# First stage of a one-core hybrid layer: a PSUM bank and a row buffer for each modulation block, the square-root table ahead of the tokens, two tiles' products side by side, and one scaling moved at the end

## The chip, the core and the metric

The kernel runs on one core of a Trainium2 chip. The metric is the device time of one execution in microseconds (us), and the kernel before takes 1265.78 us (median of 3 runs, 1265.62 to 1266.16). Everything is float32 at the interface. A matrix product is made of three products of rounded halves (high by high, high by low, low by high), so that three matmuls stand for one.

## What is computed

One layer of a diffusion backbone over 1024 latent tokens (8 tiles of 128) and 256 context tokens (2 tiles), model width 1024. The part that matters here is the beginning and the end:

```python
sh_a, sc_a, g_a, sh_f, sc_f, g_f = split(silu(c) @ w_ada + b_ada, 6)      # latent modulation
csh_a, csc_a, ...               = split(silu(c_ctx) @ w_ada + b_ada, 6)   # context modulation
hc = rmsnorm(ctx, norm_mix) * (1 + csc_a) + csh_a
hx = rmsnorm(x,   norm_mix) * (1 + sc_a)  + sh_a
u  = h @ w_in                      # its columns feed gates, attention q/k/v, mLSTM q/k/v/o
...                                # mLSTM heads, window attention, output projection
x  = x + g_f * conv_glu(modulate(rmsnorm(x, norm_ffn), sh_f, sc_f))
return rmsnorm(x, final_norm)      # per token: x / rms(x) * final_norm
```

## The kernel before, in words

**First stage** (lines 354 to 449; PE, DVE, ACT, POOL and SP follow the order of the source here, since all five are scheduled by hand). Tiles 0 and 1 are context, 2 to 9 latent. For each tile, `x_load` (L218) issues a load of 512 KB; `x_norm` squares and sums on ACT (L222), takes a root on ACT (L223) and scales on DVE (L224, L225); `x_trans` transposes on PE (L233), four blocks into each of two PSUM tiles `pt`; `x_evac` copies them into `xT`, the first half on ACT and the second on DVE (L238). Meanwhile the modulation is made in four blocks of 512 columns, numbered 0 and 1 (the two halves of the shift) and 2 and 3 (the two halves of the scale). A block is loaded in two pieces of 1 MB (`ada_load`, L258), multiplied in two steps (`ada_mm`, L269, q = 0 and 1), copied as four row groups from PSUM to the buffer `arow` by ACT (L271), and turned into columns by `ada_vec` with four small products (L278), after which DVE writes `modS` (blocks 0, 1) or `modG` (blocks 2, 3) (L281, L284).

`modulate(half, grp)` applies scale and shift to half of the eight 128-row slices of `xT`, for the context tiles (grp 0), latent tiles 2 to 5 (grp 1) or 6 to 9 (grp 2). It makes a rounded high part on ACT (L301, `hc` or `hl`), the full value on DVE or POOL (L298) and the low remainder on DVE (L303). `px_mm(c, K)` then multiplies tile c by the 272 columns `w_x`, for the slices of K0 = (1, 3, 0, 2) or K1 = (5, 7, 4, 6): for each slice high by high (L307), high by low (L308), low by high (L309). `px_out` takes the result away (L336 to L343). `spin(n)` (L352) issues n transposes whose result nobody reads.

Where things lie: `pas` holds the modulation's PSUM. Blocks 0 and 2 share one tile `pa` of two banks, and blocks 1 and 3 the next tile in the same place; products of tiles 6 and 7 are put into it too (`pas[-1]`). `arow` is one buffer for all four blocks. The pool `pl` has four banks for `pt`, `spin` and the products of tiles 2 to 5, 8 and 9. PE, ACT, DVE and POOL each run their instructions in order. DMAs are issued by SP in order, all on one queue.

**End** (the last product of the down projection, `m3`, four token blocks with 512 columns each). For block i, `after_m3` scales and adds the residual on DVE (L1956, L1484), squares on ACT (L1960) and takes a root (L2010). `end1` takes the reciprocal on DVE (L1967), scales columns 512 to 1023 on DVE (L1968) and 0 to 511 on ACT (L1969), and issues two output DMAs (L1972); one of the last block's two is issued by ACT itself. The list `plan` (L2078 to L2080) says what is issued after which block of matmuls (L2020).

Of the kernel before, what the change touches and what calls it, by code (L numbers as in the profile page):

```python
# [18 lines left out]
P = 128  # L19
D = 1024  # L20
KT = D // P
SEQ = 1024
# [56 lines left out]
def build(tc, I, out, dbg=None):  # L79
# [56 lines left out]
    def hsl(part, kt, c):  # L136
        if c < NC:
            return hc[part][:, kt, c * P:(c + 1) * P]
        c -= NC
        return hl[c // 4][part][:, kt, c % 4 * P:(c % 4 + 1) * P]  # L140
# [36 lines left out]

    pdk, pkk, plk, pa_ = (ExitStack() for _ in range(4))
    pd = pdk.enter_context(tc.tile_pool(name="pd", bufs=2, space=PSUM, side="right"))
    pk = pkk.enter_context(tc.tile_pool(name="pk", bufs=1, space=PSUM))  # L180
    pl = plk.enter_context(tc.tile_pool(name="pl", bufs=4, space=PSUM))
    xp = p1.enter_context(tc.tile_pool(name="xp", bufs=2))
# [11 lines left out]

    arow = ym[:, 1]
    scp = ym[:, 2, 0:32 * KT].rearrange("p (k j) -> p k j", k=KT)
# [65 lines left out]
    def ada_mm(n, q):  # L262
        if q == 0:
            if n in (0, 1):
                pas[-1] = pk.tile([P, SEQ], F32, name="pa", tag="pp")
            pas[n] = pas[-1][:, 512 * (n // 2):512 * (n // 2) + 512]
        pa, wa = pas[n], wps.pop((n, q))
        for k in range(4):
            T.matmul(pa[32 * k:32 * k + 32], scp[:, 4 * q + k], wa[:, k, :], start=q == 0, stop=q == 1)  # L269
        if q == 1:  # L270
            S.copy(arow, pa)  # L271

    was, wps = {}, {}

    def ada_vec(n):
        pm = pas[n][:, 0:8]
        for j in range(4):
            T.matmul(pm[:, 2 * j:2 * j + 2], arow[:, j * P:(j + 1) * P], sel[:], start=True, stop=True)  # L278
        half, dst = n % 2, (modS, modG)[n // 2]
        k4 = slice(4 * half, 4 * half + 4)  # L280
        V.tensor_tensor(out=dst[:, k4], in0=pm[:, 0:8].rearrange("p (j c) -> p j c", j=4),  # L281
                        in1=bc(spc(("bsh_a", "bsc_a")[n // 2], 4 * half, 4), 2), op=ALU.add)
        if n >= 2:
            V.scalar_tensor_tensor(out=dst[:, k4], in0=dst[:, k4], scalar=1.0, in1=bc(spc("nmix", 4 * half, 4), 2),  # L284
                                   op0=ALU.add, op1=ALU.mult)
# [35 lines left out]

    def px_mm(c, kts):
        if c not in pxs:
            if c in (6, 7):

                pxs[c] = pas[-1][:, 512 * (c - 6):512 * (c - 6) + 512]
            else:
                pool, tag = (pl, "l") if c >= 2 else (pd, "d")
                pxs[c] = pool.tile([P, 512], F32, name="px", tag=tag)
        px = pxs[c]  # L330
        for kt in kts:
            mm3(px[:, :XW], hsl(0, kt, c), hsl(1, kt, c), wX[0][:, kt, :], wX[1][:, kt, :], kt == K0[0], kt == K1[-1])

# [20 lines left out]
    with tc.manual_schedule(engines={mybir.EngineType.PE, mybir.EngineType.DVE, mybir.EngineType.Activation,  # L354
                                     mybir.EngineType.Pool}):
        with tc.manual_schedule(engines={mybir.EngineType.SP}):
            for c in range(6):
                x_load(c)
# [16 lines left out]
            x_trans(5); x_evac(5)  # L375
            ada_load(1, 0); ada_load(1, 1)
            wXf, wX = wX, wX((0,))
            ada_vec(0)
            spin(12)
            ada_mm(2, 0)  # L380
            ada_mm(2, 1)
            spin(5)
            ada_load(3, 0); ada_load(3, 1)
# [4 lines left out]
            modulate(0, 0)  # L388
            px_mm(0, K0)
            px_mm(1, K0)  # L390
            modulate(0, 1)
            x_norm(6)
            px_mm(2, K0)
            px_mm(3, K0)
            x_norm(7)
            x_trans(6); x_evac(6)
            ada_mm(1, 0)
            x_norm(8)
            x_trans(7); x_evac(7)
            x_norm(9)  # L400
            ada_mm(1, 1)
            x_trans(8); x_evac(8)
            ada_vec(1)
            ada_mm(3, 0)
# [44 lines left out]
        px_out(9)  # L449
    p0.close()  # L450


# [1512 lines left out]
    def end1(b):  # L1965
        o, r = os_[b], rn[b][:, 0:1]
        V.reciprocal(r, r)  # L1967
        V.scalar_tensor_tensor(out=o[:, 512:D], in0=o[:, 512:D], scalar=r, in1=fnr[:, 512:D], op0=ALU.mult, op1=ALU.mult)  # L1968
        S.activation(o[:, 0:512], o[:, 0:512], AF.Copy, scale=r)  # L1969
        for ns in halves[::-1]:  # L1970
            e = S if b == 3 and ns.start == 0 else nc.sync
            e.dma_start(out[b * P:(b + 1) * P, ns], o[:, ns])  # L1972
# [53 lines left out]
    for t, (p, ps, fresh) in enumerate(products):  # L2026
# [47 lines left out]
        if p == "m4":  # L2074

            part = lambda f_, *bs: [lambda b=b: f_(b) for b in bs]
            todo = [None] + todo
            plan = [todo[1:3], part(size2, 4, 5) + todo[3:4], part(size2, 6) + part(end2, 4, 5) + todo[4:5],  # L2078
                    part(size2, 7) + part(end2, 6) + part(after_m3, 0), part(end2, 7) + part(after_m3, 1) + part(end1, 0),
                    part(after_m3, 2) + part(end1, 1), part(after_m3, 3) + part(end1, 2, 3)]  # L2080
            todo = []
# [101 lines left out]
```

## Time and profile before

| what | value |
|---|---|
| time, median of 3 runs | 1265.78 us |
| time of the profiled execution | 1265.89 us |
| its span | 1264.1 us |
| PE busy | 1234.4 us (98%) |
| DVE, ACT, POOL busy | 972.8, 637.9, 187.1 us |
| first matmul starts | 9.39 us |
| last matmul ends | 1256.59 us |

The profile is of one execution. A row of the timeline gives start, length, engine, line, operation and how many instructions were merged; what stands in brackets is idle time before the row and what ended it. A matmul's length contains its way through the array, so that the distance from start to start is what a chain of matmuls pays for each. A row of the waits gives the time waited in all, how often, and the longest. A row of the DMA issues gives the median time from issue to landing.

### The profile page before, as it was taken

Reading aid. Unit: us, or ns where it says so; the run is one execution under the profiler, and the core shown is the slowest. Engines: PE = TensorE matmul, PEld = TensorE weight load, DVE = VectorE, ACT = ScalarE, POOL = GpSimd, SP = SyncE. Lnnn points to the kernel's source line nnn. Section 1 sums busy time; section 2 is a strip of 40 time slices with the busy share of each in tenths; the row PEclk is TensorE's granted clock in tenths of the full one; section 3 lists DMA queues with packets and bytes.
Section 4 is the critical chain, followed back from the end, with each engine's and each line's share of the span. In section 5 each row is a group of like instructions: output and inputs, shape, how many; then the busy total and the mean of one; then the engine's idle time right before and its main releaser. Section 6 shows DMA issues by size and latency. Waiting matters only on the chain.

```text
span 1264.1 us, 19253 instructions
## 1 busy us (share of the span) xinstructions
PE 1234.4 (98%) x7047; PEld 1060.2 (84%) x7047; DVE 972.8 (77%) x1691; ACT 637.9 (50%) x1309; POOL 187.1 (15%) x162
## 2 busy tenths in 40 slices
PE   6999999999999999999999999999999999999997
PEld 4799999999898888888887888888888888788886
DVE  5873777777787888788987877777777777877887
ACT  6632556464865777776843333333333334434435
POOL 1200000000001443221002232133231232001000
PEclk9999999999999999999999999999999999999999
DMA  9541535362354333104313322223322237975553
GB/s 361 184 142 34 145 115 153 115 181 75 85 175 160 134 120 115 51 34 167 117 51 130 115 99 102 95 102 117 103 105 100 93 135 269 335 250 187 195 192 134
DMA packets 90560, 176.17 MB, mean 139 GB/s; under 512 B 12954, under 2 KB 29538, under 8 KB 90466
## 3 DMA queue, kind: packets, MB, share of 16 engines
q1 hardware_dynamic: 90178, 174.15, 41.2%
q8 instruction: 56, 0.92, 0.3%
q10 hardware_dynamic: 288, 0.79, 0.2%
q14 instruction: 38, 0.31, 0.1%
HBM read 136.58 MB, written 38.33 MB: 138 GB/s over the span
## 4 chain that ended last, share of the span: by engine, by line
PE 84%; DVE 6%; ACT 5%; DMA 3%; issue 2%; POOL 1%; SPq 0%; ACTq 0%; DVEq 0%; POOLq 0%
PE pd L2020 14%; PE pa L1480 8%; PE pc L1480 8%; PE pp L588 7%; PE pe L1480 4%; PE pd L1480 4%; PE pb L1480 4%; PE u L1182 3%; PE pv L307 2%; PE pv L309 2%; PE pv L308 2%; PE po L307 2%; PE po L309 2%; PE po L308 2%; PE pt L1159 2%
## 5 line engine op out<-in xcount | busy, mean ns | idle before, releaser
L1597 ACT CAST wh<-Rb 128x1024 fp32r<-128x1024 f32 (+1 forms) x63 | 56.8, 903 | 144.1 <-PE pd L1480 77.1
L2020 PE MATMUL pd<-dh,al 128*128 128x512 f32 x296 | 115.4, 390 | 0.9 <-DVE al L1361 0.9
L2020 PE MATMUL pd<-dl,ah 128*128 128x512 f32 x296 | 115.3, 389 | 0.0
L2020 PE MATMUL pd<-dh,ah 128*128 128x512 f32 x296 | 115.1, 389 | 0.0
L1480 PE MATMUL pc<-hB,wh 128*128 128x512 f32 x344 | 105.6, 389 | 0.0
L1480 PE MATMUL pa<-hB,wh 128*128 128x512 f32 x336 | 103.8, 390 | 0.2 <-ACT sn L1679 0.2
L1198 DVE TENSOR_TENSOR wl<-Rb,wh 128x1024 fp32r<-128x1024 f32 (+1 forms) x63 | 65.8, 1045 | 39.2 <-ACT wh L1597 38.6
L1715 POOL TENSOR_TENSOR tt<-vt,tt 128x512 f32<-128x512 f32 x22 | 29.5, 1341 | 367.5 <-ACT tt L1709 367.5
L588 PE MATMUL pp<-hl,wh 128*128 128x512 f32 x256 | 79.3, 405 | 0.0
L307 PE MATMUL pv<-wh,hl 128*128 128x256 f32 x256 | 75.9, 296 | 0.0
L1480 PEld LDWEIGHTS pc<-hB,wh 128*128 128x128 f32 x344 | 64.6, 188 | 13.5
L1480 PEld LDWEIGHTS pa<-hB,wh 128*128 128x128 f32 x336 | 62.9, 188 | 14.1 <-ACT sn L1679 1.1
L309 PE MATMUL pv<-wh,hl 128*128 128x256 f32 x256 | 72.4, 283 | 0.0
L308 PE MATMUL pv<-wl,hl 128*128 128x256 f32 x256 | 72.3, 282 | 0.0
L2020 PEld LDWEIGHTS pd<-dh,al 128*128 128x128 f32 x296 | 55.6, 188 | 13.1 <-DVE al L1361 1.6
L1480 PE MATMUL pc<-hB,wl 128*128 128x512 f32 x172 | 66.4, 389 | 0.0
L2020 PEld LDWEIGHTS pd<-dl,ah 128*128 128x128 f32 x296 | 55.5, 188 | 11.8 <-DVE dl L1361 0.3
L1480 PE MATMUL pa<-hB,wl 128*128 128x512 f32 x168 | 65.4, 389 | 0.0
L2020 PEld LDWEIGHTS pd<-dh,ah 128*128 128x128 f32 x296 | 55.6, 188 | 11.6
L1166 ACT CAST ph<-pt 128x512 fp32r<-128x512 f32 (+1 forms) x88 | 46.2, 525 | 25.3 <-PE pt L1159 25.0
L1136 DVE TENSOR_REDUCE nm<-sps 128x1 f32<-128x641 f32 (+1 forms) x64 | 50.3, 786 | 4.9 <-PE sps L1132 3.4
L1480 PE MATMUL pd<-hB,wh 128*128 128x512 f32 x176 | 54.0, 390 | 0.0
(1082 smaller groups left out, 3694.4 us busy)
## 6 DMA issues: line engine op xcount, KB each, us to landing
w<-in_w_ada_dram SPq DMA_DIRECT2D x64, 256.0 KB, 2.8
br<-in_w_down_dram SPq DMA_DIRECT2D x25, 512.0 KB, 5.9
ar<-act_s SPq DMA_DIRECT2D x44, 256.0 KB, 4.0
Ra<-in_w_up_dram SPq DMA_DIRECT2D x21, 512.0 KB, 3.6
Rb<-in_w_up_dram SPq DMA_DIRECT2D x21, 512.0 KB, 3.6
act_a<-tt SPq DMA_DIRECT2D x33, 256.0 KB, 2.0
act_s<-tt SPq DMA_DIRECT2D x33, 256.0 KB, 2.0
wr<-in_w_h_dram SPq DMA_DIRECT2D x16, 512.0 KB, 4.1
```

The costliest lines, as they stand in the source:

```text
L307: T.matmul(ps, st_hi, mv_hi, start=first, stop=False)
L308: T.matmul(ps, st_hi, mv_lo, start=False, stop=False)
L309: T.matmul(ps, st_lo, mv_hi, start=False, stop=last)
L588: T.matmul(pp[:, 512 * n:512 * n + 512], wkq[sw][:, kt, cs], hl[n][part][:, kt, :], start=kt == 0 and sw + part == 0, stop=kt == KT - 1 an ...
L1136: V.tensor_reduce(out=self.nm[:, j:j + 1], in_=self.sv[j], axis=AX.X, op=ALU.max, negate=True)
L1166: S.copy(self.ph[i][:, :w], self.pt[i][:, :w])
L1182: T.matmul(self.u[:], vv[:, c, self.g], part[i][:, kk * 2 * P:(kk + 1) * 2 * P], start=kb + m == 0, stop=kb == last and m == 1)
L1198: sub = lambda e, o, x, y: e.tensor_tensor(out=o, in0=x, in1=y, op=ALU.subtract)
L1480: T.matmul(ps[:, cols], wt[sw][:, j, kt * P:kt * P + P], hB[part][:, blk, kt, cols], start=first and n == 0, stop=last and n == len(seq) - ...
L1597: S.copy(wt[0][:], src)
L1715: G.tensor_tensor(out=self.tt[:, h2_], in0=self.vt[:], in1=self.tt[:, h2_], op=ALU.mult)
L2020: T.matmul(ps[:], ac[sa][:, js], w[sw], start=first and n == 0, stop=last and n == 2, skip_group_check=not fresh)
```

## The change

Five edits, the first four in the first stage. (1) `pas[n]` becomes a one-bank tile of a new pool `pm_`, with one bank for blocks 0 and 1 and one for 2 and 3; tiles 6 and 7 take these banks over. Pool `pl` moves to the right side; pool `pk`, which held `pa`, is opened after the stage. (2) Block 2 gets its own row buffer. (3) An ACT activation with a square root stands ahead of the first tile. (4) The order on PE and DVE changes: `ada_vec(0)` and the first step of block 2 come before DVE's split of `w_x`, the number of spins falls from 12 + 5 to 8 + 6, two tiles are multiplied side by side (`px_two`), and blocks 1 and 3 are multiplied at other places between the transposes. (5) In the end, ACT's scaling is issued ahead of DVE's in `end1`, and `end1` of block 2 ahead of `after_m3` of block 3.

```diff
+    pm_ = pmk.enter_context(tc.tile_pool(name="pm_", bufs=1, space=PSUM))
+    pl = plk.enter_context(tc.tile_pool(name="pl", bufs=4, space=PSUM, side="right"))
...
-    arow = ym[:, 1]
+    arow = lambda n: ym[:, 7 if n == 2 else 1]
...
         if q == 0:
-            if n in (0, 1):
-                pas[-1] = pk.tile([P, SEQ], F32, name="pa", tag="pp")
-            pas[n] = pas[-1][:, 512 * (n // 2):512 * (n // 2) + 512]
+            pas[n] = pm_.tile([P, 512], F32, name="pa", tag=f"pa{n // 2}")
...
-                pxs[c] = pas[-1][:, 512 * (c - 6):512 * (c - 6) + 512]
+                pxs[c] = pas[2 * c - 11]
...
+    def px_two(cs, kts):
+        for kt in kts:
+            for c in cs:
+                px = px_bank(c)
+                T.matmul(px, hsl(0, kt, c), wX[0][:, kt, :], start=kt == K0[0], stop=False)
+                T.matmul(px, hsl(0, kt, c), wX[1][:, kt, :], start=False, stop=False)
+        for kt in kts:
+            for c in cs:
+                T.matmul(px_bank(c), hsl(1, kt, c), wX[0][:, kt, :], start=False, stop=kt == K1[-1])
...
+            S.activation(rstd[:, 0:1], spc("c4"), AF.Sqrt, bias=eps_t[:], scale=0.0)
             for c in range(6):
                 x_load(c)
...
             ada_load(1, 0); ada_load(1, 1)
+            ada_vec(0)
+            ada_mm(2, 0)
             wXf, wX = wX, wX((0,))
-            ada_vec(0)
-            spin(12)
-            ada_mm(2, 0)
+            spin(8)
             ada_mm(2, 1)
-            spin(5)
+            spin(6)
...
-            px_mm(0, K0)
-            px_mm(1, K0)
+            px_two((0, 1), K0)
             modulate(0, 1)
             x_norm(6)
-            px_mm(2, K0)
-            px_mm(3, K0)
+            px_two((2, 3), K0)
             x_norm(7)
+            ada_mm(1, 0)
             x_trans(6); x_evac(6)
-            ada_mm(1, 0)
             x_norm(8)
+            ada_mm(1, 1)
             x_trans(7); x_evac(7)
             x_norm(9)
-            ada_mm(1, 1)
+            ada_vec(1)
             x_trans(8); x_evac(8)
-            ada_vec(1)
             ada_mm(3, 0)
...
     p0.close()
+    pmk.close()
+    pk = pkk.enter_context(tc.tile_pool(name="pk", bufs=1, space=PSUM))
...
         V.reciprocal(r, r)
+        S.activation(o[:, 0:512], o[:, 0:512], AF.Copy, scale=r)
         V.scalar_tensor_tensor(out=o[:, 512:D], in0=o[:, 512:D], scalar=r, in1=fnr[:, 512:D], op0=ALU.mult, op1=ALU.mult)
-        S.activation(o[:, 0:512], o[:, 0:512], AF.Copy, scale=r)
...
-                    part(after_m3, 2) + part(end1, 1), part(after_m3, 3) + part(end1, 2, 3)]
+                    part(after_m3, 2) + part(end1, 1), part(end1, 2) + part(after_m3, 3) + part(end1, 3)]
```

Outside the places shown below, and the swap on DVE of block 0's `modS` with the split of `w_x`, each engine's instructions stand in the same order as before, to the end of the program; SP's order is the same throughout.

PE, where tiles 0 and 1 meet, before (`hc0` is the high part, `hc1` the low remainder; `px` with its number is the tile's PSUM):

```order
L307 MATMUL px_431<-wh_364,hc0_178 128x272
L308 MATMUL px_431<-wl_365,hc0_178 128x272
L309 MATMUL px_431<-wh_364,hc1_179 128x272
L307 MATMUL px_444<-wh_364,hc0_178 128x272
L308 MATMUL px_444<-wl_365,hc0_178 128x272
L309 MATMUL px_444<-wh_364,hc1_179 128x272
```

The same engine after, at the last slice of the high parts:

```order
L339 MATMUL px_430<-wh_375,hc0_178 128x272
L340 MATMUL px_430<-wl_376,hc0_178 128x272
L339 MATMUL px_433<-wh_375,hc0_178 128x272
L340 MATMUL px_433<-wl_376,hc0_178 128x272
L343 MATMUL px_430<-wh_375,hc1_179 128x272
L343 MATMUL px_433<-wh_375,hc1_179 128x272
```

Before, each slice's three products stand together and the second tile follows the first; after, the tiles alternate, and all products with the low remainder stand behind all those with the high part.

PE between the products of tile 3 and those of tile 4, before (`pt` transposes of tiles 6 to 9; `pa<-wa` block 1, `pa<-sel` its `ada_vec`, `pa<-wt` block 3):

```order
L233 MATMUL pt<-ident,xi 128x128 x8
L269 MATMUL pa<-wa,ym 32x512 x4
L233 MATMUL pt<-ident,xi 128x128 x8
L269 MATMUL pa<-wa,ym 32x512 x4
L233 MATMUL pt<-ident,xi 128x128 x8
L278 MATMUL pa<-sel,ym 128x2 x4
L269 MATMUL pa<-wt,ym 32x512 x4
L233 MATMUL pt<-ident,xi 128x128 x8
```

The same place after:

```order
L267 MATMUL pa<-wa,ym 32x512 x4
L233 MATMUL pt<-ident,xi 128x128 x8
L267 MATMUL pa<-wa,ym 32x512 x4
L233 MATMUL pt<-ident,xi 128x128 x8
L276 MATMUL pa<-sel,ym 128x2 x4
L233 MATMUL pt<-ident,xi 128x128 x8
L267 MATMUL pa<-wt,ym 32x512 x4
L233 MATMUL pt<-ident,xi 128x128 x8
```

Both steps of block 1 moved one tile ahead, `ada_vec(1)` stands ahead of tile 8, and tile 8 now lies between `ada_vec(1)` and the first step of block 3.

ACT at the very end, before (o_11163 is block 2 and o_11164 block 3; `jk` is the sum of squares):

```order
L1969 ACTIVATE o_11162<-o_11162,rn_11170 128x512
L1960 ACTIVATE jk_12767,rn_11172<-o_11164 128x512
L2010 ACTIVATE rn_11172<-rn_11172 128x1
L1969 ACTIVATE o_11163<-o_11163,rn_11171 128x512
L1969 ACTIVATE o_11164<-o_11164,rn_11172 128x512
```

After (o_11167 is block 2, o_11168 block 3):

```order
L1980 ACTIVATE o_11166<-o_11166,rn_11174 128x512
L1980 ACTIVATE o_11167<-o_11167,rn_11175 128x512
L1972 ACTIVATE jk_12776,rn_11176<-o_11168 128x512
L2022 ACTIVATE rn_11176<-rn_11176 128x1
L1980 ACTIVATE o_11168<-o_11168,rn_11176 128x512
```

The scaling of block 2 moved ahead of block 3's squares; DVE's reciprocal and scaling of block 2 move in the same way ahead of block 3's residual.

More of the change, by code (lines that the diff above doesn't have):

```diff
@@ L175, in load_split @@
         return rest
-    pdk, pkk, plk, pa_ = (ExitStack() for _ in range(4))
+    pdk, pkk, plk, pa_, pmk = (ExitStack() for _ in range(5))
     pd = pdk.enter_context(tc.tile_pool(name="pd", bufs=2, space=PSUM, side="right"))
-    pk = pkk.enter_context(tc.tile_pool(name="pk", bufs=1, space=PSUM))
-    pl = plk.enter_context(tc.tile_pool(name="pl", bufs=4, space=PSUM))
+    pm_ = pmk.enter_context(tc.tile_pool(name="pm_", bufs=1, space=PSUM))
+    pl = plk.enter_context(tc.tile_pool(name="pl", bufs=4, space=PSUM, side="right"))
     xp = p1.enter_context(tc.tile_pool(name="xp", bufs=2))
@@ L270, in ada_mm @@
         if q == 1:
-            S.copy(arow, pa)
+            S.copy(arow(n), pa[:])
     was, wps = {}, {}
@@ L277, in ada_vec @@
         for j in range(4):
-            T.matmul(pm[:, 2 * j:2 * j + 2], arow[:, j * P:(j + 1) * P], sel[:], start=True, stop=True)
+            T.matmul(pm[:, 2 * j:2 * j + 2], arow(n)[:, j * P:(j + 1) * P], sel[:], start=True, stop=True)
         half, dst = n % 2, (modS, modG)[n // 2]
@@ L320, in rotate, with px_bank @@
         V.tensor_tensor(out=sv(dst), in0=sv(dst), in1=sv(ta[:])[:, :, ::-1], op=ALU.add)
-    def px_mm(c, kts):
+    def px_bank(c):
         if c not in pxs:
             if c in (6, 7):
-                pxs[c] = pas[-1][:, 512 * (c - 6):512 * (c - 6) + 512]
+                pxs[c] = pas[2 * c - 11]
             else:
@@ L329, in px_mm @@
                 pxs[c] = pool.tile([P, 512], F32, name="px", tag=tag)
-        px = pxs[c]
+        return pxs[c][:, :XW]
+    def px_mm(c, kts):
+        px = px_bank(c)
         for kt in kts:
-            mm3(px[:, :XW], hsl(0, kt, c), hsl(1, kt, c), wX[0][:, kt, :], wX[1][:, kt, :], kt == K0[0], kt == K1[-1])
+            mm3(px, hsl(0, kt, c), hsl(1, kt, c), wX[0][:, kt, :], wX[1][:, kt, :], kt == K0[0], kt == K1[-1])
+    def px_two(cs, kts):
+        for kt in kts:
+            for c in cs:
+                px = px_bank(c)
+                T.matmul(px, hsl(0, kt, c), wX[0][:, kt, :], start=kt == K0[0], stop=False)
[3 more added lines that the diff above has]
+                T.matmul(px_bank(c), hsl(1, kt, c), wX[0][:, kt, :], start=False, stop=kt == K1[-1])
     def px_out(c):
```

## The prediction

> **What bounds the kernel now.** I read the page's busy shares first, then the windows of the stages that the edits touch, then the timeline of PE there, then what it waits for, and last the end. From the page:
>
> ```profile
> PE 1234.4 (98%) x7047; PEld 1060.2 (84%) x7047; DVE 972.8 (77%) x1691; ACT 637.9 (50%) x1309; POOL 187.1 (15%) x162
> ```
>
> The windows (PE busy, number, clock, share of the DMA engines, GB/s) show where the other 2% is:
>
> ```profile
> 10.00:28.30 18.30, 16.24 (x119) 1.00 1.04 396
> 28.30:36.20 7.90, 7.62 (x49) 1.00 1.04 390
> 36.20:45.00 8.80, 8.19 (x66) 1.00 0.96 351
> 53.80:75.00 21.20, 21.20 (x167) 1.00 0.32 100
> ```
>
> Up to 45 us the DMA engines are full at 390 to 400 GB/s; from 53.8 us on PE has no hole at all. So what counts is how early PE gets into the stretch after 53.8 us: whatever it gains until then is kept, since all later work follows in an unchanged order. Before that, a product can start no earlier than its piece of the modulation weights lands. The issues on SP, and the time from issue to landing of each of these four:
>
> ```profile
> 9.51 2.38 SPq L258 DMA_DIRECT2D wa<-in_w_ada_dram  x1
> 19.78 0.38 SPq L258 DMA_DIRECT2D wa<-in_w_ada_dram  x1
> 21.55 0.92 SPq L258 DMA_DIRECT2D wa<-in_w_ada_dram  x1
> 24.26 3.23 SPq L258 DMA_DIRECT2D wt<-in_w_ada_dram  x1
> ```
>
> ```profile
> wa<-in_w_ada_dram SPq DMA_DIRECT2D x1, 1024.0 KB, 14.7
> wa<-in_w_ada_dram SPq DMA_DIRECT2D x1, 1024.0 KB, 14.8
> wa<-in_w_ada_dram SPq DMA_DIRECT2D x1, 1024.0 KB, 15.8
> wt<-in_w_ada_dram SPq DMA_DIRECT2D x1, 1024.0 KB, 15.8
> ```
>
> Issue plus landing: block 2's second piece lands at 24.2, block 1's two at 34.6 and 37.35, block 3's first at 40.1 us. PE around them:
>
> ```profile
> 23.39 1.97 PE L269 MATMUL pa<-wa,ym 128*32 128x512 f32 x16 [0.48 <-DVE modS L281]
> 26.11 1.05 PE L278 MATMUL pa<-sel,ym 128*128 128x2 f32 x8
> 27.02 0.96 PE L352 MATMUL spin<-ident 128*128 128x128 f32 x7
> 28.32 0.40 PE L307 MATMUL px<-wh,hc 128*128 128x272 f32 x1 [0.34 <-ACT hc L301]
> ...
> 36.17 1.04 PE L233 MATMUL pt<-ident,xi 128*128 128x128 f32 x8
> 37.13 1.06 PE L269 MATMUL pa<-wa,ym 128*32 128x512 f32 x8
> 38.13 1.09 PE L233 MATMUL pt<-ident,xi 128*128 128x128 f32 x8
> 39.15 1.06 PE L269 MATMUL pa<-wa,ym 128*32 128x512 f32 x8
> 40.15 1.09 PE L233 MATMUL pt<-ident,xi 128*128 128x128 f32 x8
> 41.31 1.05 PE L278 MATMUL pa<-sel,ym 128*128 128x2 f32 x8
> 42.69 1.07 PE L269 MATMUL pa<-wt,ym 128*32 128x512 f32 x8 [0.33 <-DVE modS L281]
> 43.69 1.09 PE L233 MATMUL pt<-ident,xi 128*128 128x128 f32 x8
> 45.02 0.40 PE L307 MATMUL px<-wh,hl 128*128 128x272 f32 x1 [0.24 <-ACT xT L238]
> ```
>
> Block 2 (23.39) ends at 25.36: its second half of about 1.0 us starts at 24.3, as the weights land. Block 1's second step starts at 39.15, 1.8 us after its weights: there PE is late, not the DMA.
>
> **The change, part by part.** *Root table ahead.* The load that it takes away from between the first two tiles, and the hole in which it now lies:
>
> ```profile
> 5.59 1.06 ACT L222 ACTIVATE ym<-xi 128x1024 bf16<-128x1024 f32 x1 [2.43 <-DMA xi<-in_ctx_dram]
> ...
> 6.76 1.28 ACT L223 ACT_TABLE_LOAD   x1
> ```
>
> ACT waits 2.43 us for the first tile, which holds the 1.28 us load and one small activation. So the six tiles run 1.28 us earlier; but block 2 cannot end before 24.2 + 1.0 us, and it does so already. I count 0; without that cover it would be 1.28 us.
>
> *Own bank and row buffer, block 2's first step and `ada_vec(0)` ahead.* They take away the 0.48 us at 23.39. Block 2's first step now runs when its first piece lands, but the second ends at 25.3 as before. Again 0, with at most 0.1 us of gain. The three spins that go away stood in waits; the new row buffer's first other use is a DVE write after the products at 26.11 that read it. Nothing is lost there. PE will stand idle for about 1.3 us ahead of block 2's first piece and 0.7 us ahead of the second. The Trainium skill ("TensorE: Matmul & The Clock Gate", What's actually happening) says that the array falls to half its clock after an idle window of about 3.4 us; by that rule these holes cost nothing either, and the sum stays.
>
> *Two tiles side by side.* Before, the 48 products of tiles 0 to 3 go from 28.32 to 36.17, 7.85 us. Their pace without a wait, here also across a change of bank:
>
> ```profile
> 53.63 0.28 PE L309 MATMUL pa<-wh,hl 128*128 128x272 f32 x1
> 53.75 0.29 PE L307 MATMUL px<-wh,hc 128*128 128x272 f32 x1
> ```
>
> That is 0.125 us from start to start, 6.0 us for 48. What they wait for is the low remainder, once for each slice, first by DVE's own row and then by PE's waits:
>
> ```profile
> 31.89 2.48 DVE L303 TENSOR_TENSOR hl<-ym,hl 128x512 fp32r<-128x512 f32 x4
> ```
>
> ```profile
> PEld px L309 <- DVE hl L303: 1.2, 6, 0.3
> PEld pa L269 <- DMA wa<-in_w_ada_dram: 0.7, 1, 0.7
> ```
>
> The last remainder of tiles 2 and 3 is there at 31.89 + 2.48 = 34.37. Before, it feeds tile 2's last product, and all twelve of tile 3 (1.5 us) follow: 36.17. After, only two products of that slice are left, since the 16 with the high part run while DVE works: 34.37 + 0.04 + 2 x 0.125 = 34.65. Gain: 1.5 us. An alternation between two banks at every second product is not in the trace. Its pace is bounded by the 0.125 us above, and by the slow pace that PE shows at its start:
>
> ```profile
> 9.39 3.67 PE L233 MATMUL pt<-ident,xi 128*128 128x128 f32 x16 [9.39 <-DVE xi L225]
> 15.47 1.06 PE L233 MATMUL pt<-ident,xi 128*128 128x128 f32 x8 [0.51 <-DVE xi L225]
> ```
>
> There a transpose takes 0.23 us, later 0.13: 1.75 times as long, which would make 0.22 us of 0.125. I take 0.125, since one change of bank costs nothing; the other end is the third rival. A rule of the Trainium skill speaks for that other end (the same page, A second HAM failure mode: psum-queue depth-cycling): a kernel that cycles through PSUM banks lets PE stop so often that its clock falls again and again.
>
> *Order of blocks 1 and 3.* Step by step, with lengths from the rows above (a step or a tile's transposes 1.0 us from start to start, `ada_vec` 0.9): block 1's first step 34.65 (its weights landed at 34.6), tile 6 at 35.65 to 36.65. Then PE waits: the second step must not start before 37.4. What is queued behind it is all that follows on PE, tile 7 first; ACT and DVE wait for tiles 7 to 9. From there: tile 7 at 38.4, `ada_vec(1)` at 39.4, tile 8 at 40.3, block 3's first step at 41.3 (weights at 40.1), tile 9 at 42.2, where before it was 43.69. So 1.5 us are gained at tile 9, and the wait at 42.69 (0.33 us) is gone within this. Tile 9's second half waits perhaps 0.2 us for DVE's copy of tile 8, which now stands behind `modS`; ACT copies the first half, which releases tile 4's product: 45.02 - 1.5 = 43.5. From tile 4 on the order is the old one. Later, tile 6 no longer waits for `modG` (0.33 us before); but the products of tiles 2 and 3 with K1 wait for DVE's remainders, which hang on `modG` and moved by the same 1.5 us. So that bit is given back. The first stage gains 1.5 us, at least 1.0 (tile 9 late on DVE, or weights 0.4 us later) and at most 1.75 (39.15 to 37.4).
>
> *The end.* ACT's last rows, with the wait ahead of block 3's squares, DVE's first of block 3, and the landing of ACT's DMA:
>
> ```profile
> 1258.06 0.63 ACT L1960 ACTIVATE jk<-o 128x512 bf16<-128x512 f32 x1 [1.74 <-DVE o L1484]
> ...
> 1259.02 1.32 ACT L1969 ACTIVATE o<-o,rn 128x512 f32<-128x512 f32 x2
> 1260.37 0.37 ACTq L1972 DMA_DIRECT2D out_dram<-o  x1
> ```
>
> ```profile
> 1256.61 0.69 DVE L1956 TENSOR_TENSOR tm<-pd,gfr 128x512 f32<-128x512 f32 x1 [1.12 <-PE pd L2020]
> ```
>
> ```profile
> out_dram<-o ACTq DMA_DIRECT2D x1, 256.0 KB, 2.8
> ```
>
> The two scalings (1.32) are blocks 2 and 3; block 2's now lies in the hole of 1.74 us, and DVE's part of it (0.9 us) in that of 1.12 us. Block 3's can start when its reciprocal is there, some 0.3 us earlier (1259.3 instead of 1259.6). The last DMA then starts 0.3 us earlier, and the two of block 2 are out of its way. I count 0.35 us, between 0.1 (block 2's DVE part delays block 3's by 0.2) and 0.7 (the last landing at 2.3 instead of 2.8 us). The swap inside `end1` orders two engines that do not wait for each other: 0.
>
> *Sum.* The profiled execution took 1265.89 us, 0.11 more than the median. 1265.89 - 1.5 - 0.35 = 1264.04, less 0.11: **1263.9 us**.
>
> **The rivals.**
> - *The DMA queue does follow.* If the loads were bound by their issue, the 1.28 us of the root table would move all landings, and the caps at 24.2 and 37.35 with them: 1263.9 - 1.28 = 1262.6. For it: block 1's first load is issued (19.78) as soon as block 0's product has freed the buffer. Against it: the loads land 15 us after issue with the DMA engines at 1.04 all the while. 0.11.
> - *The lead is lost.* If a chain on DVE or ACT in the later stages, and not PE, sets the pace at some place, only the 0.35 us at the end and little else remain: 1265.4. Against it: 21.20 of 21.20 us busy from 53.8 on, and later DVE's inputs come from PE's products, which are early too. 0.16.
> - *PE falls to its slow pace in the side-by-side products*, which makes it slower. At 0.22 us, 48 products take 10.6 us and end at 38.9 instead of 34.65. Block 1's first step and tile 6 follow, so its second step starts at 40.9, or 41.4 if these two are slow in part; before, it was 39.15. 1265.8 + 2.0 - 0.35 = 1267.4; each further step of 1.0 us at the slow pace adds 0.75, so from the second on it is slower by over 0.2%. It decides from about half of the products on: the first 0.7 us fall into the wait for block 1's weights, and 1.85 more eat the gain. Against it: PE kept its pace over the present waits of this stretch (six of 0.3 us or less). The rule of the Trainium skill on cycling through banks (the page and section above) would give this time; this trace shows the slow pace at the start alone. 0.07.
>
> **How the numbers follow.** My forecast has 0.66. Its own bounds are -1.75 - 0.7 and -1.0 - 0.1: 1263.2 to 1264.8, to which 0.2 us for the spread of the runs comes. The range reaches over the lost lead, to 1265.5, and at the low side to 1262.9, a little short of the first rival (0.11); left out are that rival and the slow pace, 0.18 together, and what I do not see. A change of 0.2%, about what a measurement can tell, is 2.5 us: faster than 1263.25 are the first rival and a small part of the forecast (0.11 + 0.07), slower than 1268.3 most of the slow pace (0.05), and 0.77 lie between.
>
> **What would show it.** Right: in the changed profile the first root needs no table load, yet block 2 still ends at 25.3; PE's products of tile 3 end near 34.7; block 1's second step starts at its landing near 37.4; tile 4 starts near 43.5; the stretch from 53.8 to 75 us is shifted by 1.5 us; ACT's last scaling starts 0.2 to 0.3 us after the root before it, with no other scaling between. Wrong: landings of the modulation weights over 0.5 us earlier, products of 272 columns 0.2 us apart in the side-by-side stretch, a lead at 75 us that is gone at 400, or block 3's residual delayed at the end.

## The result and the profile after

The changed kernel takes 1264.76 us (median of 22 runs, 1263.32 to 1266.44), the kernel before beside it 1266.31 (22 runs, 1265.62 to 1269.23). The ratio is 0.9984, 95% interval 0.9978 to 0.9990: about 2.0 us, 0.16%. The medians alone lie 1.55 us apart, the sum foresaw 1.85. It is a gain, since the interval leaves out 1, but a smaller one than the 0.2% that the prediction took for what a measurement can tell. The profiled execution took 1263.85 us (span 1262.1), where the prediction's sum for such an execution was 1264.04; it was the fourth fastest of the 22, and the median lies 0.9 us above the 1263.9 of the prediction. Between the two profiled executions lie 2.04 us: 1.69 up to the last matmul and 0.35 behind it.

The page of the changed kernel, busy times:

```profile
PE 1233.2 (98%) x7044; PEld 1059.5 (84%) x7044; DVE 973.4 (77%) x1691; ACT 638.8 (51%) x1310; POOL 187.5 (15%) x162
```

The windows of the first stretch and of the one without a hole (PE busy and number first; clock, DMA share and GB/s last):

```profile
10.00:28.30 18.30, 14.95 (x111) 9.87 (x109) 9.93 (x21) 10.76 (x22) 0.53 (x1) 1.00 1.04 396
...
53.80:75.00 21.20, 21.20 (x164) 20.63 (x163) 16.38 (x45) 8.98 (x18) 3.30 (x3) 1.00 0.33 103
```

Up to 28.3 us PE works 1.3 us less than before in the same window, and yet it is no later. Its first transposes start 1.22 us earlier (8.17 for 9.39), so that more of the work lies ahead of the window, and the lead ends as idle time ahead of weights. The timeline of PE around blocks 2, 1 and 3:

```profile
21.58 1.07 PE L267 MATMUL pa<-wa,ym 128*32 128x512 f32 x8 [1.20 <-DMA wa<-in_w_ada_dram]
22.57 1.09 PE L363 MATMUL spin<-ident 128*128 128x128 f32 x8
24.28 1.06 PE L267 MATMUL pa<-wa,ym 128*32 128x512 f32 x8 [0.61 <-DMA wa<-in_w_ada_dram]
...
28.26 0.40 PE L339 MATMUL px<-wh,hc 128*128 128x272 f32 x1 [0.34 <-ACT hc L299]
28.49 0.29 PE L340 MATMUL px<-wl,hc 128*128 128x272 f32 x1
28.62 0.29 PE L339 MATMUL px<-wh,hc 128*128 128x272 f32 x1
...
33.39 1.50 PE L343 MATMUL px<-wh,hl 128*128 128x272 f32 x8
34.97 1.06 PE L267 MATMUL pa<-wa,ym 128*32 128x512 f32 x8
35.97 1.09 PE L233 MATMUL pt<-ident,xi 128*128 128x128 f32 x8
37.60 1.07 PE L267 MATMUL pa<-wa,ym 128*32 128x512 f32 x8 [0.54 <-DMA wa<-in_w_ada_dram]
...
39.52 0.95 PE L276 MATMUL pa<-sel,ym 128*128 128x2 f32 x8
...
41.34 1.06 PE L267 MATMUL pa<-wt,ym 128*32 128x512 f32 x8
...
43.68 0.39 PE L305 MATMUL px<-wh,hl 128*128 128x272 f32 x1
```

Both steps of block 2 now wait for DMA, the second until 24.28, as before. The side-by-side products start 0.125 us apart, bank by bank. Tile 3's last product ends ahead of 34.97, and block 1's second step now has a wait in brackets, for its DMA, where before it had none: it starts at 37.60 instead of 39.15. Tile 4 starts at 43.68 instead of 45.02. The root's table, on ACT:

```profile
3.21 1.28 ACT L368 ACT_TABLE_LOAD   x1
...
5.65 1.06 ACT L222 ACTIVATE ym<-xi 128x1024 bf16<-128x1024 f32 x1 [0.85 <-DMA xi<-in_ctx_dram]
```

The load lies in ACT's wait for the first tile, of which 0.85 us is left. The end, PE's last row, then ACT's after block 3's sum of squares, and the landing of ACT's own DMA:

```profile
1254.04 0.84 PE L2032 MATMUL pd<-e0h,e0l 128*128 128x512 f32 x3
```

```profile
1257.13 0.29 ACT L2022 ACTIVATE rn<-rn 128x1 f32<-128x1 f32 x1
1257.71 0.72 ACT L1980 ACTIVATE o<-o,rn 128x512 f32<-128x512 f32 x1 [0.29 <-DVE rn L1979]
1258.46 0.38 ACTq L1984 DMA_DIRECT2D out_dram<-o  x1
```

```profile
out_dram<-o ACTq DMA_DIRECT2D x1, 256.0 KB, 2.7
```

One scaling is left behind the root, and it waits for nothing but DVE's reciprocal. Before, the same last row of PE was:

```profile
1255.73 0.84 PE L2020 MATMUL pd<-e0h,e0l 128*128 128x512 f32 x3
```

### The profile page after: what moved, and what is told of

Read it like the earlier page. It is cut to its first block, busy times and chain, and to the rows that moved or that the text cites. A ratio compares the mean times of both kernels' runs of the same rounds, so it can differ in the third digit from the quotient of the medians.

```text
span 1262.1 us, 19247 instructions
## 1 busy us (share of the span) xinstructions
PE 1233.2 (98%) x7044; PEld 1059.5 (84%) x7044; DVE 973.4 (77%) x1691; ACT 638.8 (51%) x1310; POOL 187.5 (15%) x162
## 4 chain that ended last, share of the span: by engine, by line
PE 80%; DVE 7%; ACT 5%; DMA 5%; issue 2%; SPq 1%; POOL 1%; ACTq 0%; DVEq 0%; POOLq 0%
PE pd L2032 14%; PE pa L1492 8%; PE pc L1492 8%; PE pp L600 7%; PE pe L1492 4%; PE pd L1492 4%; PE pb L1492 4%; PE u L1194 3%; PE pv L305 2%; PE pv L307 2%; PE pv L306 2%; DMA wa<-in_w_ada_dram 2%; PE pt L1171 2%; PE po L305 2%; PE po L307 1%
```

## The experiments

The theory is the prediction's: the time comes from the side-by-side products, the gain is capped where block 1's weights land, and 0.35 us come at the end. The rivals: the table ahead moves the loads; or the banks and the row buffer, or the order, carry the gain; or the idle time that PE now has ahead of block 2 costs something. "Tile 4" is the start of its first product in the profiled execution, "span" that of the same execution; ratios are to the kernel before on the same chip.

| run | median us (runs) | lowest to highest | ratio [95%] | tile 4 | span |
|---|---|---|---|---|---|
| before | 1266.31 (22) | 1265.62 to 1269.23 | 1 | 45.02 | 1264.1 |
| changed | 1264.76 (22) | 1263.32 to 1266.44 | 0.9984 [0.9978, 0.9990] | 43.68 | 1262.1 |
| table_alone | 1266.45 (10) | 1265.86 to 1267.23 | 0.9999 [0.9989, 1.0008] | 44.96 | 1264.9 |
| banks_alone | 1266.13 (10) | 1264.90 to 1267.83 | 0.9996 [0.9987, 1.0006] | 44.46 | 1263.8 |
| two_alone | 1265.30 (10) | 1264.51 to 1266.20 | 0.9991 [0.9981, 1.0000] | 44.26 | 1262.7 |
| end_alone | 1265.97 (10) | 1265.38 to 1267.79 | 0.9997 [0.9987, 1.0006] | 45.49 | 1265.0 |
| without_two | 1265.95 (10) | 1264.15 to 1267.02 | 0.9997 [0.9987, 1.0006] | 44.63 | 1264.2 |
| old_block_order | 1265.67 (10) | 1264.60 to 1266.41 | 0.9995 [0.9985, 1.0005] | 45.03 | 1264.1 |
| late_weights | 1266.28 (10) | 1265.60 to 1267.88 | 1.0000 [0.9991, 1.0010] | 45.43 | 1264.6 |
| no_spins | 1267.69 (10) | 1266.29 to 1268.91 | 1.0010 [1.0001, 1.0020] | 46.57 | 1264.5 |
| early_weights | 1264.41 (11) | 1263.62 to 1265.44 | 0.9984 [0.9976, 0.9993] | 44.42 | 1262.3 |
| early_both | 1263.61 (11) | 1262.88 to 1264.27 | 0.9979 [0.9970, 0.9988] | 43.08 | 1261.9 |
| holes_filled | 1265.86 (11) | 1264.05 to 1267.88 | 0.9998 [0.9989, 1.0007] | 43.44 | 1263.4 |
| early_both_filled | 1264.01 (11) | 1263.04 to 1264.89 | 0.9984 [0.9975, 0.9993] | 42.75 | 1261.2 |

### One part alone

**table_alone** is the kernel before with the root table ahead.

```diff
+            S.activation(rstd[:, 0:1], spc("c4"), AF.Sqrt, bias=eps_t[:], scale=0.0)
             for c in range(6):
                 x_load(c)
```

> The kernel before with the root table ahead of the tokens and nothing else. Theory (PE comes late into the stretch after 45 us, and the weights' landings cap it): the tiles run 1.3 us earlier, block 2 still ends at 25.3 us, tile 4 starts at 45.0 as before, time within 0.3 us of before. Rival (the DMA queue follows the earlier tiles): the weights of blocks 2 and 1 land about 1.3 us earlier (22.9 and 36.1 us), and the time falls by 1.3 us.

Measured: 0.9999. PE, the second step of block 2 and the place ahead of tile 4:

```profile
24.25 1.06 PE L269 MATMUL pa<-wa,ym 128*32 128x512 f32 x8 [0.88 <-DMA wa<-in_w_ada_dram]
...
42.63 1.07 PE L269 MATMUL pa<-wt,ym 128*32 128x512 f32 x8 [0.33 <-DVE modS L281]
```

The first transposes start 1.28 us earlier than before (8.11 for 9.39), and block 2's second step starts at 24.25, where before its weights were loaded into PE at 24.29. Block 1's first load was issued 0.94 us earlier (18.84 for 19.78) and yet landed at the same 34.6, 15.8 us after its issue instead of 14.8. The landings did not move, and the rival of the queue that follows falls.

**banks_alone** is the kernel before with the one-bank tiles, the second row buffer and the pools, but the old order.

```diff
+            pas[n] = pm_.tile([P, 512], F32, name="pa", tag=f"pa{n // 2}")
...
+    arow = lambda n: ym[:, 7 if n == 2 else 1]
```

> The kernel before with a bank per modulation block and the row buffer of block 2 alone, order as before. Theory: block 2's first step no longer waits for the shift's columns, but its second still ends at 25.3; block 3's first step no longer waits for them (0.33 us and its start-up), so tile 4 starts 0.3 to 0.5 us earlier (44.5 to 44.7), time 0.3 to 0.5 us less. Rival (the removed waits of 0.48, 0.33 and 0.33 us are the gain): 1.1 us less, tile 4 0.8 us earlier.

Measured: 0.9996; its interval holds 1. In its timeline the wait of 0.33 us ahead of block 3's first step is gone, and tile 4 is 0.56 us earlier, 0.16 of which was there ahead of tile 6 already:

```profile
42.14 1.07 PE L267 MATMUL pa<-wt,ym 128*32 128x512 f32 x8
```

**two_alone** is the kernel before with the side-by-side products.

```diff
-            px_mm(0, K0)
-            px_mm(1, K0)
+            px_two((0, 1), K0)
...
-            px_mm(2, K0)
-            px_mm(3, K0)
+            px_two((2, 3), K0)
```

> The kernel before with the side-by-side products of tiles 0 to 3 alone. Theory: tile 3's products end 1.2 us earlier (34.9 to 35.0 instead of 36.17), tile 6 then waits until 35.2 for its scaling on DVE, tile 4 starts at 44.1 (0.9 us earlier), time 0.9 us less. Rival (waits removed by the banks are the gain): no change at tile 4. Rival (slow pace when two banks alternate): products 0.22 us apart, tile 3's end at 38 us or later, slower by 1 us and more.

Measured: 0.9991, by the medians the largest of the four parts; the intervals of all four overlap. PE behind tile 3:

```profile
35.39 1.07 PE L233 MATMUL pt<-ident,xi 128*128 128x128 f32 x8 [0.44 <-DVE xi L225]
```

Tile 3's last product starts at 34.66 (before 36.04, in the changed kernel 34.60), but the old order has tile 6's transposes next, and those wait 0.44 us for DVE. In the new order block 1's first step stands there, with weights that have landed. Tile 4 starts 0.76 us earlier than before; of the 1.4 us half arrives.

**end_alone** is the kernel before with the two edits at the end.

```diff
-                    part(after_m3, 2) + part(end1, 1), part(after_m3, 3) + part(end1, 2, 3)]
+                    part(after_m3, 2) + part(end1, 1), part(end1, 2) + part(after_m3, 3) + part(end1, 3)]
```

> The kernel before with the two edits at the end alone. Theory: from the last matmul's end to the end of the span 0.35 us less than the 7.5 us before, nothing else moves. Rival (block 2's scaling on DVE delays block 3's residual): the residual of block 3 starts 0.1 to 0.7 us after the last matmul, and the time stays as it is or rises.

Measured: 0.9997, no difference that can be told. Its first stage came 0.47 us late in the profiled execution (weights of block 2's second step loaded into PE at 24.75, after a later landing), but the end can be measured on its own: from PE's last three matmuls, whose row stands at 1256.96, to ACT's last DMA

```profile
1261.39 0.38 ACTq L1972 DMA_DIRECT2D out_dram<-o  x1
```

are 4.43 us; in the kernel before it was 1260.37 - 1255.73 = 4.64, in the changed one 1258.46 - 1254.04 = 4.42. So the DMA starts 0.2 us earlier, where the sum had 0.3, and it lands 0.1 us sooner (2.7 for 2.8): together the 0.35 us of the sum, within the rounding.

### One part undone

**without_two** is the changed kernel with the old products.

```diff
-            px_two((0, 1), K0)
+            px_mm(0, K0)
+            px_mm(1, K0)
...
-            px_two((2, 3), K0)
+            px_mm(2, K0)
+            px_mm(3, K0)
```

> The changed kernel with tiles 0 to 3 multiplied one after the other again. Theory: tile 3's products end at 36.1 us, after the landing cap no longer matters; PE then runs block 1, tiles 6 to 8 and block 3 without a hole, tile 4 starts at about 44.3 (changed kernel 43.68, before 45.02); time 0.65 us above the changed kernel, 1.0 us below before. Rival (the order of blocks 1 and 3 gives nothing): tile 4 at 45.0.

Measured: 0.9997 where the whole change has 0.9984. PE, where block 1 is multiplied:

```profile
36.21 1.07 PE L267 MATMUL pa<-wa,ym 128*32 128x512 f32 x8
...
38.23 1.06 PE L267 MATMUL pa<-wa,ym 128*32 128x512 f32 x8
```

No step waits for its weights any more: PE is late again. Of the change's lead of 1.34 us at tile 4, 0.95 is gone (44.63 for 43.68; foreseen 44.3). So the new products are needed for most of the gain, and the cap at 37.6 is what they run into. The time rose by about 1.6 us over the change by the ratios, more than the first stage explains: in the profiled execution another 0.5 us of lead went at 326 to 328 us, where PE waits for DVE behind the read-back that holes_filled shows below.

**old_block_order** is the changed kernel with blocks 1 and 3 at their old places.

```diff
-            ada_mm(1, 0)
             x_trans(6); x_evac(6)
+            ada_mm(1, 0)
             x_norm(8)
-            ada_mm(1, 1)
             x_trans(7); x_evac(7)
             x_norm(9)
-            ada_vec(1)
+            ada_mm(1, 1)
             x_trans(8); x_evac(8)
+            ada_vec(1)
             ada_mm(3, 0)
```

> The changed kernel with blocks 1 and 3 at their old places between the transposes. Theory: with own banks the old order needs no wait for the shift's columns; tile 6 waits for its scaling at 35.2, block 1's second step starts at about 38.2, after its landing, tile 4 starts between 43.7 and 44.1: the order is worth 0 to 0.4 us. Rival (the order is the larger part of the gain): tile 4 at 44.7 or later, 1 us slower than the changed kernel.

Measured: 0.9995. The profiled execution does not isolate the order, because something else happened ahead of it (PE, rows of block 2, then of tile 6):

```profile
22.91 1.97 PE L363 MATMUL spin<-ident 128*128 128x128 f32 x8
24.81 1.73 PE L267 MATMUL pa<-wa,ym 128*32 128x512 f32 x8
...
36.54 1.06 PE L233 MATMUL pt<-ident,xi 128*128 128x128 f32 x8 [0.45 <-DVE xi L225]
```

Eight spins take 1.97 us instead of 1.09, the step 1.73 instead of 1.06. What can be read is the wait of 0.45 us ahead of tile 6, as in two_alone. How much the order is worth by itself stays open; the intervals of this run and of the change overlap.

**late_weights** is the changed kernel with two small loads issued ahead of block 1's weights instead of behind block 3's.

```diff
+            nc.sync.dma_start(rw[:], I["rw"][0:1, 0:536].broadcast_to([P, 536]))
+            nc.sync.dma_start(rope[:], I["rope"])
             ada_load(1, 0); ada_load(1, 1)
```

> The changed kernel with the loads of the row table and the rotary table (0.27 and 0.52 MB) issued ahead of block 1's weights instead of behind block 3's, so that blocks 1 and 3 land about 2.0 us later. Theory: block 1's second step starts at its landing, 39.6, tile 4 starts at about 45.6, and the time rises by 1.9 us over the changed kernel, to that of before. Rival (PE or ACT sets the pace there, not the landing): less than 0.5 us.

Measured: 1.0000. PE:

```profile
22.62 1.97 PE L363 MATMUL spin<-ident 128*128 128x128 f32 x8
24.52 1.81 PE L267 MATMUL pa<-wa,ym 128*32 128x512 f32 x8
...
39.35 1.06 PE L267 MATMUL pa<-wa,ym 128*32 128x512 f32 x8 [0.54 <-DMA wa<-in_w_ada_dram]
```

Block 1's second step waits for weights that land 1.75 us later, and tile 4 comes at 45.43, 1.75 us later: 6.08 us behind the second step in both kernels. The slow spins occur here too, but they end well ahead of this wait. The landing of block 1's second piece is the cap of the changed kernel.

### The idle time ahead of block 2

**no_spins** is the changed kernel without its three rows of spins.

```diff
-            spin(8)
             ada_mm(2, 1)
-            spin(6)
...
-            spin(7)
             modulate(0, 0)
```

> The changed kernel without any of its 21 remaining spins. Theory: they stand in waits only; holes of 1.2 and 1.7 us ahead of block 2's two steps and about 1 us behind do not change the pace; products of 272 columns stay 0.125 us apart from 28.3 us on, time within 0.3 us of the changed kernel. Rival (PE falls to its slow pace without them): products 0.22 us apart for some us, tile 3's end at 36 us or later, time up by 1 to 3 us.

Measured: 1.0010 [1.0001, 1.0020], slower than before, and 2.6 thousandths above the changed kernel. PE and, for a stretch of 9 us, the window with its clock (PE, PEld, DVE, ACT, POOL, then PEclk):

```profile
24.65 1.94 PE L267 MATMUL pa<-wa,ym 128*32 128x512 f32 x8 [1.62 <-DMA wa<-in_w_ada_dram]
27.29 1.87 PE L276 MATMUL pa<-sel,ym 128*128 128x2 f32 x8 [0.70 <-ACT ym L269]
...
30.32 0.59 PE L339 MATMUL px<-wh,hc 128*128 128x272 f32 x1 [1.16 <-ACT hc L299]
30.71 0.43 PE L340 MATMUL px<-wl,hc 128*128 128x272 f32 x1
```

```profile
24.00:33.00 9.00, 6.49 (x28) 4.67 (x29) 3.58 (x10) 3.92 (x7) 3.17 (x4) 0.50 1.03 399
```

The granted clock is 0.50. Everything on PE takes nearly twice as long; the products go 0.22 us apart. All ten executions had a mean clock of 0.993 to 0.995, none of the changed kernel's one below 0.997. The spins are no idle filler: without them the clock falls every time.

**early_weights** lets the loads of block 2 and 1 go ahead of half of `w_x`.

```diff
             ada_load(2, 0); ada_load(2, 1)
-            wX.load(1)
...
             ada_load(1, 0); ada_load(1, 1)
+            wX.load(1)
```

> The changed kernel with the second half of w_x (0.54 MB) loaded behind block 1's weights instead of ahead of tiles 6 to 9. Theory: block 1's weights land 1.35 us earlier (33.5 and 36.2), its second step no longer waits (0.54 us), tile 4 starts at 43.1 instead of 43.68, time 0.5 us below the changed kernel. Rival (ACT and DVE set the pace of tiles 6 to 9): tile 4 within 0.15 us of 43.68.

Measured: 0.9984, the same as the change. PE, and the window:

```profile
21.81 1.82 PE L267 MATMUL pa<-wa,ym 128*32 128x512 f32 x8 [1.20 <-DMA wa<-in_w_ada_dram]
23.57 1.96 PE L363 MATMUL spin<-ident 128*128 128x128 f32 x8
25.46 1.06 PE L267 MATMUL pa<-wa,ym 128*32 128x512 f32 x8
...
38.02 1.07 PE L267 MATMUL pa<-wa,ym 128*32 128x512 f32 x8
```

```profile
22.00:25.00 3.00, 3.00 (x15) 1.44 (x8) 0.33 (x1) 0.00 (x0) 0.00 (x0) 0.50 1.04 397
```

Block 1's second step does not wait any more: the cap is gone. But in this execution the clock fell behind the hole of 1.20 us, block 2's second step began 1.2 us later than in the changed kernel, and what the earlier weights gave was spent. The times do not show that this alone cost the gain: the six executions with a mean clock of 0.999, too high for such a fall (see holes_filled), took 1264.24 us on average, no less than the profiled one.

**early_both** also moves the first half of `w_x` behind block 2's loads, and its split behind `ada_vec(2)`.

```diff
-            wX = load_split(I["w_x"], XW, split=False, alloc=False, now=(0,))
             ada_load(2, 0); ada_load(2, 1)
+            wX = load_split(I["w_x"], XW, split=False, alloc=False, now=(0,))
...
             ada_vec(2)
+            wXf, wX = wX, wX((0,))
```

> As early_weights, and the first half of w_x loaded behind block 2's weights, split behind block 2's columns. Theory: block 2's weights land 1.35 us earlier and its columns are there at about 25.9 instead of 27.2; the split of w_x then stands between on ACT and DVE (1.1 and 1.3 us), so that DVE's remainders gain only some 0.5 us: tile 3's products end at about 34.4, tile 4 starts at about 42.6, time 1.0 us below the changed kernel. Rival (the split in the chain costs as much as the weights gain): no better than early_weights, or slower.

Measured: 0.9979 [0.9970, 0.9988], the lowest median of all. PE:

```profile
20.62 1.06 PE L267 MATMUL pa<-wa,ym 128*32 128x512 f32 x8
...
23.23 1.07 PE L267 MATMUL pa<-wa,ym 128*32 128x512 f32 x8 [0.53 <-DMA wa<-in_w_ada_dram]
...
36.68 1.06 PE L267 MATMUL pa<-wa,ym 128*32 128x512 f32 x8
```

The hole of 1.2 us ahead of block 2's first step is gone, the clock stays up, and tile 4 starts 0.6 us earlier than in the changed kernel (43.08; foreseen 42.6). It beats the kernel before; its interval overlaps that of the change, so that it beats the change as well is likely by the medians and not shown.

**holes_filled** is the changed kernel with spins in both holes.

```diff
+            spin(11)
             ada_mm(2, 0)
...
-            spin(8)
+            spin(14)
```

> The changed kernel with 11 spins ahead of block 2's first step and 14 instead of 8 ahead of its second, so that PE has no hole of more than about 0.2 us between 18 and 25.3 us. Theory (in most executions of the changed kernel PE falls to its slow pace behind the 1.2 us hole ahead of block 2, which costs 1.2 us): block 2's steps take 1.0 us and the spins 0.11 us apart, the first product of 272 columns starts 4.0 us after block 2's second piece lands, median about 1263.7, ratio to before 0.998, no run as slow as the slower half of the changed kernel's (1264.75 and more). Rival (the executions differ by something else, the landings for one): median near 1264.8, ratio 0.9987, spread as in the changed kernel.

Measured: 0.9998. The first stage of the profiled execution went as the theory of the holes expects: no slow row, tile 4 at 43.44. The time did not: nine of the eleven runs lie above 1264.75, where none was foreseen. In the profiled execution (1265.14) the lead went at 320 to 327 us. The timeline of holes_filled there: DVE's row that waits for a load, SP's row that issues it, and PE's row that waits for DVE:

```profile
325.35 0.76 DVE L676 TENSOR_TENSOR ee<-ee,tri 128x256 f32<-128x256 f32 x2 [3.15 <-DMA ee<-m_d]
```

```profile
319.85 0.89 SPq L660 DMA_DIRECT2D ee<-m_d  x2
```

```profile
326.37 0.33 PE L666 MATMUL pn<-ident,kT 128*128 128x128 f32 x1 [2.26 <-DVE cst L701]
```

of the changed kernel:

```profile
323.80 0.76 DVE L675 TENSOR_TENSOR ee<-ee,tri 128x256 f32<-128x256 f32 x2 [1.32 <-DMA ee<-m_d]
```

```profile
320.12 0.89 SPq L659 DMA_DIRECT2D ee<-m_d  x2
```

```profile
324.82 0.33 PE L665 MATMUL pn<-ident,kT 128*128 128x128 f32 x1 [0.43 <-DVE cst L700]
```

and PE's row of the kernel before:

```profile
326.57 0.33 PE L653 MATMUL pn<-ident,kT 128*128 128x128 f32 x1 [0.73 <-DVE cst L688]
```

`ee` is a row of decays that is read back from device memory, 256 KB, and DVE's mask on it stands in DVE's order ahead of the copy `cst` that PE needs. In holes_filled the load is issued 0.27 us earlier than in the changed kernel, but DVE gets it 5.5 us after the issue instead of 3.7, and PE is 1.55 us later behind it. In all the other profiled executions, the kernel before among them (issued 321.59, used 325.56), it took 3.6 to 4.0 us. So a lead of 1.74 us over the kernel before (issue at 321.59 there) shrinks to 0.20 (PE's row at 326.57) in one step. Why that load took longer this once is open.

It does not account for the median. Every run also has a mean granted clock. In the ten profiles in which the clock did not fall in the first stage, it falls only at the very end, behind PE's last work, and the mean is 0.998 or 0.999; for 0.997 it must be at half for 6.3 us or more, longer than any of those ends (at most 5.3 us). With a fall of 3.4 us besides an end (2.3 us at least) 0.999 cannot be reached. The five runs of holes_filled with 0.999, the profiled one among them, took 1264.05 to 1265.20 us; the other six, five with 0.997 and one with 0.998, took 1265.86 to 1267.88. So in at least five the clock fell somewhere in the kernel, although the holes ahead of block 2 were filled. Where it fell no profile shows, nor that this alone made these runs slower.

**early_both_filled** is early_both with 13 spins in place of 8.

```diff
-            spin(8)
+            spin(13)
```

> early_both with 13 instead of 8 spins ahead of block 2's second step, which fills its hole of 0.53 us; no hole of PE is left before block 2 ends. Theory: early_both has no hole of over 0.6 us in this stretch and already keeps the quick pace, so it stays at 1263.6 within 0.4 us; against before 2.4 to 2.8 us. Rival (a hole of 0.5 us is enough to lose the pace in some executions): 0.3 to 0.6 us faster than early_both, spread smaller.

Measured: 0.9984; tile 4 at 42.75, the shortest span of all (1261.2), and no difference from early_both that the runs can tell. Its mean clock was 0.998 or 0.999 in all eleven runs, as in early_both. With no hole over 0.6 us left, more spins had nothing to save.

## Why the prediction came out right, step by step

- **Root table: 0.** Right: table_alone 0.9999, landings where they were.
- **Side by side: 1.5 us at tile 3, pace 0.125 us.** Right: the products go 0.125 us apart over the two banks, tile 3's last one starts 1.44 us earlier (36.04 to 34.60), and block 1's step follows at 34.97 (foreseen 34.65; its weights landed at 34.9, issue at 18.89 plus 16.0 us, 0.3 us later than before). The slow pace of the third rival did not appear there, in any of the profiles with spins. The rule on cycling through banks that spoke for it (the Trainium skill, "TensorE: Matmul & The Clock Gate", A second HAM failure mode: psum-queue depth-cycling) had nothing to act on: PE did not stop between the groups.
- **Order of the blocks: cap at 37.4, tile 4 at 43.5.** Right: 37.60 and 43.68, 1.34 us gained of 1.5 foreseen. The missing 0.2 is the landing, 37.55 (21.55 plus 16.0) where the sum took 37.35; late_weights shows that the cap is the landing. That the order carries a part is not shown by itself.
- **Own bank and row buffer: 0.** Right in the sum, but alone they are worth some 0.4 us at tile 4, most of it the wait of 0.33 us that the prediction had put under the order. In the changed kernel it lies under the cap.
- **The end: 0.35 us.** Right, in the changed kernel and alone.
- **"By that rule these holes cost nothing either, and the sum stays."** This is the step that does not hold, though the profiled execution obeyed it. In three of the five profiles that have the hole of 1.2 us and the spins behind it (early_weights, late_weights, old_block_order) the granted clock fell to 0.50 behind it, and block 2 took 0.9 to 1.0 us longer from its first step to its columns (5.4 us for 4.47); in none of the eight profiles that have no such hole. In the changed kernel 0.54 us of that would fall into the wait for block 1's weights. By the mean clocks seven of its 22 runs (0.997) had a fall somewhere, and ten (0.999) had none; the seven took 1264.92 us on average and the ten 1264.26, but the fastest run of all is among the seven. A mean of 0.997 or less also stands at 17 of all 63 runs of the kernels with the hole and the spins, at 5 of 11 of holes_filled, and at 8 of the 166 others without the hole, 104 of them of the kernel before. So the hole goes with more falls, but it is not their only cause.
- **"Whatever it gains until then is kept."** Kept in the changed kernel: SP's issue of `ee` is 1.47 us earlier (321.59 to 320.12), the last matmuls 1.69. But the first stage gave only 1.34: at the first `px<-wh,hc` behind it the lead is 1.33 (53.75 to 52.42), after the waits for DVE's remainders had taken back what the wait of 0.33 us for `modG` gave, as foreseen. The other 0.36 came later, in waits that happened to be shorter, such as 0.43 us for 0.73 at `cst`. From one profiled execution to another, what the later stages add to the lead over the kernel before lies between -1.2 and +0.8 us, so that the close agreement of 1263.85 with 1264.04 is in part luck. The gain holds only while the waits of later stages stay as they are. The load of `ee` releases PE there through DVE, and the one execution in which it took 5.5 us lost 1.5 us. The second rival, a lead lost later to a chain on DVE, thus has its place, though the changed kernel's profile did not fall into it.
- **Slips that change nothing.** The DMA engines were full only up to 36.2 us; in the window behind it their share was 0.96, at 351 GB/s. By its own steps tile 9 starts at 42.3 and not 42.2 (measured 42.38). From 1265.78 its own bounds come to 1263.3 and 1264.7, not 1263.2 and 1264.8.

So the two costs that the sum left out, the clock and a late read-back, did not strike the changed kernel's profiled execution; in executions of its near relatives they cost 0.9 to 1.0 us and 1.5 us at their places.

## What to carry to other kernels

A gain on PE ends at the next landing: look up when the input of the step behind it arrives, and if it caps the gain, move its load ahead of one that is needed later (early_both did). Before a filler on PE is called idle work, look at what PE does in the few microseconds around each hole; a hole of 1.2 us beside two-column products was enough here to halve the clock in some executions. Read the mean clock of every run beside its time: it tells apart runs that one profile cannot. And where a read-back from device memory stands ahead of a busy engine's next instruction, a lead is not safe until it is past that place.

## What the runs showed of the hardware that was not expected

Taking the clock of single microseconds and counting what lies below 1.00 as half speed, it stayed at 0.50 for 3.4 us in early_weights, late_weights and old_block_order, and for 10.24 us, three times as long, in no_spins. The window of early_weights ahead of the fall:

```profile
18.40:21.80 3.40, 2.21 (x20) 1.80 (x16) 1.69 (x4) 2.14 (x3) 0.00 (x0) 1.00 1.05 388
```

PE had worked 2.21 of these 3.40 us when the clock fell at 22.0; the missing 1.19 us are the one hole ahead of 21.81. Each of these four executions has a second fall, behind PE's last work. It comes 1235.6 us after the first in early_weights and no_spins and 1239.0 us after it in the other two, one stretch of 3.4 us more. So the falls lie on a grid that runs on through the execution, whatever PE does. With steps of 3.413 us (a third of 10.24), 1235.6 us are 362 steps. Counted back as many from the fall at the end of the changed kernel (1258.84), its hole lies within one step, too:

```profile
19.80:23.21 3.41, 2.21 (x20) 1.29 (x20) 1.98 (x3) 0.97 (x1) 0.00 (x0) 1.00 1.04 385
```

PE was busy just as long there, and the clock stayed at 1.00. So the busy time of the profile does not decide. What differs between the five profiles is what stands beside the hole: the steps that ended in a fall hold all of `ada_vec(0)`, whose products have two columns each (0.95 us), those of the changed kernel and of without_two only the last 0.58 and 0.48 us of it. That such products hardly count as work for the clock would fit all five; no run tests it.

The Trainium skill ("TensorE: Matmul & The Clock Gate", What's actually happening) tells of half the clock in free-running windows of 3413 ns; the half, the length and the free running agree with these runs. That the clock falls only after an idle window does not, if idle means a window without work: here a window with PE busy for two thirds was enough. Where the hole falls on the grid would also explain why it strikes some executions and not others; that is argued, not shown.
